# A second load in channel-by-token layout for the later channel steps of a transformer layer

## The chip, the cores and the metric

The kernel runs on one core of one Trainium2 chip. The metric is device time in microseconds (us) of one execution; the time before is the median of three runs. A profile of one execution shows each engine's instructions: TensorE (PE, with its weight loads as PEld), VectorE (DVE), ScalarE (ACT), GpSimd (POOL), and SyncE (SP), which only issues transfers. 16 DMA engines carry the transfers.

## The reference

One layer of a diffusion backbone in float32: 256 latent tokens `x` and 256 context tokens `ctx`, 2048 channels each. What matters here is the beginning:

```python
m_lat = [m[:, None, :] for m in adaln(c, w_ada[l], b_ada[l])]      # silu(c) @ w_ada + b_ada, six chunks
m_ctx = adaln(c_ctx, w_ada[l], b_ada[l])
hc = modulate(rms_norm(ctx, norm1_g[l]), m_ctx[0], m_ctx[1])       # h * (1 + scale) + shift
pc = hc @ w_in_l[:, :KV_WIDTH]                                     # keys and values of the context
h = modulate(rms_norm(x, norm1_g[l]), m_lat[0], m_lat[1])
p = h @ w_in_l                                                     # keys, values, queries, gates
```

`rms_norm` multiplies each token by its own reciprocal root of the mean square, and each channel by a gain. `modulate` multiplies each channel by 1 + scale and adds shift; both depend on the channel and on whether the token is latent or context, not on the token. After this come two kinds of attention, gates, an output projection and a SwiGLU block, which the change does not touch.

## The kernel before, in words

Tokens stand in four blocks of 128: blocks 0 and 1 are context, 2 and 3 latent. Channels stand in 16 tiles of 128 (`kt`). Products are made in three passes (`mm3`, L211 to L214): each float32 operand is split into a rounded part `hi` and a rest `lo`, and hi·hi, hi·lo and lo·hi are added up. For the product the channels must lie on the partitions, so each token tile is turned.

**Loads (L93 to L96).** `tok_in[q]` holds 512 channels of all four blocks, token by channel. SP's queue also carries every weight load: `load_w` (L198 to L209) loads two tiles of 128 rows into a `wraw` buffer, ACT rounds it to `whi` (L207), DVE makes the rest `wlo` (L208). `ada_cond` (L251 to L289) loads 512 KB pieces of `w_ada` (`wada`), multiplies them on PE with 32 columns (L268), and gives scale and shift of some channel tiles. `wraw` and `wada` share seven buffers, so SP waits when all seven are in use.

**Startup (L524 to L541).** For each block in the order 2, 3, 0, 1: `row_norm` (L131) sums squares on ACT and DVE and lets POOL take the power -0.5 (`rstd_of`, L124 to L129); `row_scale` (L145) multiplies the block's first 512 channels by the result on DVE; channel tile 0 is turned, modulated (`mod_first`) and multiplied with some of `w_in`. Then the other 1536 channels of the block are scaled (L539).

**Steps (L523, L544 to L572).** `steps = [(0, 1), (1, 1), (2, 2), (4, 4), (8, 4), (12, 4)]` are pairs of first channel tile and count. In each step, `kv_group` (L355 to L381) multiplies the step's tiles of all four blocks with six groups of 512 columns of `w_in` (keys and values), adding up in SBUF (L378 on DVE). Between the groups, the scale and shift for the next step are made, and after the last two groups `modulated` (L295 to L320) prepares the next step's channels: PE turns two channel tiles of two blocks into one PSUM tile `xtp` (L309, four transposes), DVE (L314) and ACT (L316) each modulate one tile into `hx`, ACT rounds both (`hi`) and DVE subtracts (`lo`, L218). The latent part goes to `xT`, which stays for the queries and gates, the context part to `cT`. From the last two groups of step 3 on, DVE also adds up other `w_ada` chunks (`ada_pieces`, L395).

**Order.** Buffers come from pools: `big` has 15 tiles of 1 MB (128 x 2048 float32) for `tok_in`, the key and value sums, `xT` and `cT`; `tp` is two PSUM banks for everything that is turned; `scr` three scratch tiles. Each engine runs its queue in order. That order is made at build time by a planner: the text's order is the priority, and an instruction whose inputs and buffers are ready may be placed ahead of earlier ones that still wait. `tc.issue_after(i)` keeps instructions of an engine behind `i`, as for `small_loads` (L548 to L550), which are on POOL's queue.

Of the kernel before, what the change touches and what calls it, by code (L numbers as in the profile page):

```python
# [11 lines left out]
F32 = mybir.dt.float32  # L12
F32R = mybir.dt.float32r
AF = mybir.ActivationFunctionType
ALU = mybir.AluOpType
AX = mybir.AxisListType

P = 128
D = 2048
NKT = D // P  # L20
SEQ = 256
# [13 lines left out]
CG = 512  # L35
# [10 lines left out]
def hybrid_block(ctx: ExitStack, tc: tile.TileContext, t: dict, out: bass.AP):  # L46
    nc = tc.nc
# [3 lines left out]
    tab = ctx.enter_context(tc.tile_pool(name="tab", bufs=1))  # L51
# [5 lines left out]
    def big_tile(name, dt=F32):  # L57
        return big.tile([P, 2048], dt, tag="big", name=name)
# [4 lines left out]
    def tp_ps(name="tp"):  # L63
        return psum.tile([P, CG], F32, tag="tp", bufs=2, name=name)
# [4 lines left out]
    def scratch(name, n=CG, dt=F32, tag="scr", bufs=3):  # L69
        return scr.tile([P, n], dt, tag=tag, bufs=bufs, name=name)  # L70

    def small(name, n):
        return sm.tile([P, n], F32, tag=f"sm{n}", name=name)


    ident = tab.tile([P, P], F32, name="ident")
# [3 lines left out]
    ones = tab.tile([P, 32], F32, name="ones")  # L80
# [40 lines left out]

    last_pow = []

    def rstd_of(ss, n, dim, name, by=1.0):  # L124

        r = small(name, n)
        nc.vector.tensor_scalar(out=r, in0=ss, scalar1=by / dim, scalar2=EPS * by, op0=ALU.mult, op1=ALU.add)
        last_pow.append(nc.gpsimd.tensor_tensor(out=r, in0=r, in1=neghalf[:, 0:n], op=ALU.pow))
        return r  # L129

    def row_norm(i):  # L131
        ssq = small("ss_part", 4)
        for q in range(4):
            xt = tok_in[q][:, i, :]
            junk = scratch("junk", tag="p", bufs=4)
            if q % 2 == 0:
                nc.scalar.activation(out=junk, in_=xt, func=AF.Square, accum_out=ssq[:, q:q + 1])
            else:
                nc.vector.scalar_tensor_tensor(out=junk, in0=xt, scalar=1.0, in1=xt, op0=ALU.mult, op1=ALU.mult,
                                               accum_out=ssq[:, q:q + 1])  # L140
        ss = small("ss_row", 1)
        nc.vector.tensor_reduce(out=ss, in_=ssq, axis=AX.X, op=ALU.add)
        return rstd_of(ss, 1, D, "rstd_row")

    def row_scale(i, r, qs):  # L145
        for q in qs:
            xt = tok_in[q][:, i, :]
            nc.vector.tensor_scalar(out=xt, in0=xt, scalar1=r, scalar2=None, op0=ALU.mult)

    def small_loads():  # L150

        def to_all(dst, nm):
            nc.gpsimd.dma_start(out=dst, in_=t[nm].partition_broadcast(P).rearrange("p l d -> p (l d)"))

        lamv = scratch("lamv", 4 * BD, tag="p", bufs=4).rearrange("p (i c) -> p i c", i=4)
        for i, nm in enumerate(("lam_q1", "lam_q2", "lam_k1", "lam_k2")):
            to_all(lamv[:, i, :], nm)
        gsub = tab.tile([P, BV], F32, name="gsub")
        to_all(gsub, "subln_g")
        gains, cosin = {}, {}  # L160
        for br, hd, tag in (("a", AD, "sq"), ("b", BD, "nr")):
            cosin[br] = scratch("cs", 2 * hd, tag="p", bufs=4).rearrange("p (i w c) -> p i w c", i=2, w=2)
            nc.gpsimd.dma_start(out=cosin[br], in_=t[f"rope_{br}"].rearrange("(i p) w c -> p i w c", p=P))
            gains["k" + br] = tab.tile([P, hd], F32, name=f"g_k{br}")
            gains["q" + br] = scratch("gq", hd, tag=tag, bufs=2)
            for qk in ("q", "k"):
                to_all(gains[qk + br], f"{qk}_norm_{br}")
        return lamv, gsub, gains, cosin
# [47 lines left out]
    def split(hi, lo, src):  # L216
        nc.scalar.copy(out=hi, in_=src)
        nc.vector.tensor_tensor(out=lo, in0=src, in1=hi.bitcast(F32), op=ALU.subtract)  # L218
# [24 lines left out]
    xT = Parts("xT", NKT)  # L243
# [51 lines left out]
    def modulated(k0, nk):  # L295

        shift, scale = cond_of[k0]
        cT = big_tile("cT", F32R).rearrange("p (h k c) -> p h k c", h=2, c=CTX)
        cT_of[k0] = cT
        for w in range(2):  # L300
            for j in range(0, nk, 2):
                tp = tp_ps("xtp")
                hx = scratch("hx")
                m = min(2, nk - j)
                for jj in range(m):
                    kt = k0 + j + jj
                    for i in range(2):
                        c0 = (2 * jj + i) * P
                        nc.tensor.transpose(out=tp[:, c0:c0 + P], identity=ident,  # L309
                                            in_=tok_in[kt // 4][:, i + 2 - 2 * w, (kt % 4) * P:(kt % 4 + 1) * P])  # L310
                    sl = slice(jj * SEQ, (jj + 1) * SEQ)
                    s_c, b_c = scale[:, j + jj, w:w + 1], shift[:, j + jj, w:w + 1]
                    if jj == 0:
                        nc.vector.tensor_scalar(out=hx[:, sl], in0=tp[:, sl], scalar1=s_c, scalar2=b_c, op0=ALU.mult, op1=ALU.add)  # L314
                    else:
                        nc.scalar.activation(out=hx[:, sl], in_=tp[:, sl], func=AF.Identity, scale=s_c, bias=b_c)  # L316
                kt = k0 + j
                v, k = (xT.tile4(kt // 4), kt % 4) if w == 0 else (cT, j)
                split(v[:, 0, k:k + m, :], v[:, 1, k:k + m, :], hx[:, 0:m * SEQ].rearrange("p (k c) -> p k c", k=m))
                yield None  # L320

    firsts, last_first = {}, []

    def keep_busy(n):

        idle = mm_ps("idle")
        with tc.issue_after(last_pe[0].ins):
            for _ in range(n):
                nc.tensor.transpose(out=idle[:, 0:P], in_=ident, identity=ident)
# [18 lines left out]
    def kv_first(tok, cg):  # L348
        (hi, lo), (wh, wl) = firsts[tok], ws0[cg]
        nm, idx = kv_of[cg]  # L350
        ps = mm_ps()
        last_pe[0] = mm3(ps, hi, lo, wh[:, 0], wl[:, 0], True, True)
        nc.scalar.copy(out=acc[nm][idx][:, tok * CG:(tok + 1) * CG], in_=ps)
# [136 lines left out]
    def take(gen, n):  # L490
        for _ in range(n):
            if next(gen, gen) is gen:
                return

    def drain(gen):
        for _ in gen:
            pass
# [32 lines left out]
    for tok, todo in ((2, ((2, 2),)), (3, ((3, 2), (2, 3), (3, 3), (2, 0), (3, 0))), (0, ((0, 2), (0, 3), (0, 0))), (1, ((1, 2), (1, 3), (1, 0)))):  # L530
        r = row_norm(tok)
        row_scale(tok, r, (0,))
        if tok >= 2:
            keep_busy(16 if tok == 2 else 8)
        mod_first(tok)
        if tok >= 2:
            keep_busy(10)
        with tc.issue_after(last_first[-1].ins):
            row_scale(tok, r, (1, 2, 3))  # L539
        for of in todo:  # L540
            kv_first(*of)  # L541
    later = ada_later()
    later_keys = iter(())
    for si, (k0, nk) in enumerate(steps):  # L544
        last = si == len(steps) - 1
        nxt = iter(()) if last else ada_cond(*steps[si + 1])
        mod = iter(()) if last else modulated(*steps[si + 1])
        if si == 2:  # L548
            with tc.issue_after(last_pow[3].ins):
                lamv, gsub, gains, cosin = small_loads()  # L550
        if si == 4:
            with tc.issue_after(last_lo[-1].ins):
                lambdas()
            tables()
        if last:
            later_keys = keys("b", 0)
        for n, cg in enumerate((2, 3, 0, 4, 5, 1)):
            if si == 0 and cg in ws0:
                continue
            for half, _ in enumerate(kv_group(si, k0, nk, cg)):  # L560
                if half == 0 and n in BATCH[si]:
                    take(nxt, 1)
                if si == 3 and n >= 4:
                    take(later, 2)
                elif si > 3:
                    take(later, 1)
                if last and n > 0:
                    take(later_keys, 1)
            if n >= 4:
                drain(nxt)  # L570
                take(mod, 2)
        drain(mod)  # L572
# [144 lines left out]
    def unit(br, u):  # L717
        return (u // 4, u % 4) if br == "a" else (u // 8, u // 2 % 4)
# [59 lines left out]
    for n, (br, u) in enumerate(units):  # L778
        q = (br, unit(br, u)[0])
# [33 lines left out]
    for cg in range(4):  # L813
        m, gs = [], []
# [194 lines left out]
```

## Time and profile before

| what | value |
| --- | --- |
| median of 3 runs | 1733.82 us (1732.61 to 1733.86) |
| span of the profiled execution, first to last instruction | 1730.7 us |
| time outside that span, against the median | 3.1 us |
| PE busy, share of the span | 1706.1 us, 99% |
| DVE busy | 1132.6 us, 65% |
| ACT busy | 775.0 us, 45% |
| DMA moved | 397.69 MB, mean 230 GB/s |
| transposes of the changed steps | 48, between 109.8 and 273.8 us |

The span runs from the first to the last instruction of the profiled execution; the runs' time also holds what lies around it. Busy time of PE is modelled at its end, so the start of one instruction to the start of the next is the better price of an instruction there. "idle before" names the time an engine did nothing, and what ended it. A stretch in the tables is given in us from the span's start.

### The profile page before, as it was taken

Reading aid. Unit: us, or ns where it says so; the run is one execution under the profiler, and the core shown is the slowest. Engines: PE = TensorE matmul, PEld = TensorE weight load, DVE = VectorE, ACT = ScalarE, POOL = GpSimd, SP = SyncE. Lnnn points to the kernel's source line nnn. Section 1 sums busy time; section 2 is a strip of 40 time slices with the busy share of each in tenths; the row PEclk is TensorE's granted clock in tenths of the full one; section 3 lists DMA queues with packets and bytes.
Section 4 is the critical chain, followed back from the end, with each engine's and each line's share of the span. In section 5 each row is a group of like instructions: output and inputs, shape, how many; then the busy total and the mean of one; then the engine's idle time right before and its main releaser. Section 6 shows DMA issues by size and latency. Waiting matters only on the chain.

```text
span 1730.7 us, 21827 instructions
## 1 busy us (share of the span) xinstructions
PE 1706.1 (99%) x8150; PEld 1378.5 (80%) x8150; DVE 1132.6 (65%) x1428; ACT 775.0 (45%) x1063; POOL 135.5 (8%) x204
## 2 busy tenths in 40 slices
PE   7999999999999999999999999999999999999998
PEld 5667778887787788888888788888888888888887
DVE  5754668888788879796665754555565665454554
ACT  5222223245656556667544444444444444333332
POOL 2100001001131120002110100000000000000000
PEclk9999999999999999999999999999999999999999
DMA  9877785687766676777796766677777777666662
GB/s 263 300 242 265 233 319 174 201 271 235 252 189 202 212 265 217 247 227 248 249 323 222 237 180 190 201 237 241 234 242 234 240 236 231 208 213 197 221 205 88
DMA packets 192010, 397.69 MB, mean 230 GB/s; under 512 B 13504, under 2 KB 25872, under 8 KB 191392
## 3 DMA queue, kind: packets, MB, share of 16 engines
q1 hardware_dynamic: 183952, 369.71, 66.2%
q0 software_dynamic: 7952, 26.58, 4.8%
q8 instruction: 64, 1.05, 0.2%
q14 instruction: 42, 0.34, 0.1%
HBM read 385.72 MB, written 10.52 MB: 229 GB/s over the span
## 4 chain that ended last, share of the span: by engine, by line
PE 88%; DVE 5%; issue 3%; DMA 1%; ACT 1%; POOL 1%; SPq 0%; DVEq 0%; ACTq 0%; POOLq 0%
PE mm L212 26%; PE mm L213 26%; PE mm L214 26%; PE ada L268 2%; DVE wlo L208 1%; PE ptp L687 1%; PE o L705 1%; DMA wraw<-in_w_in_dram 1%; PE ftp L951 1%; PE s L667 1%; ACT whi L207 1%; PE o L213 0%; PE o L214 0%; PE o L212 0%; PE s L212 0%
## 5 line engine op out<-in xcount | busy, mean ns | idle before, releaser
L208 DVE TENSOR_TENSOR wlo<-wraw,whi 128x1024 fp32r<-128x1024 f32 (+1 forms) x506 | 611.6, 1210 | 460.2 <-ACT whi L207 458.8
L207 ACT CAST whi<-wraw 128x1024 fp32r<-128x1024 f32 (+1 forms) x506 | 527.7, 1043 | 796.6 <-PE mm L214 682.0
L213 PE MATMUL mm<-wlo,hT 128*128 128x512 f32 x696 | 271.0, 389 | 2.0 <-DVE wlo L208 2.0
L212 PE MATMUL mm<-whi,hT 128*128 128x512 f32 x696 | 272.8, 392 | 0.0
L214 PE MATMUL mm<-whi,hT 128*128 128x512 f32 x696 | 271.3, 390 | 0.1
L212 PE MATMUL mm<-whi,xT 128*128 128x512 f32 x640 | 257.2, 404 | 0.6 <-ACT whi L207 0.6
L213 PE MATMUL mm<-wlo,xT 128*128 128x512 f32 x640 | 251.5, 393 | 0.9 <-DVE wlo L208 0.9
L214 PE MATMUL mm<-whi,xT 128*128 128x512 f32 x640 | 250.5, 392 | 0.0
L213 PEld LDWEIGHTS mm<-wlo,hT 128*128 128x128 f32 x696 | 130.7, 188 | 28.8 <-DVE wlo L208 2.4
L214 PEld LDWEIGHTS mm<-whi,hT 128*128 128x128 f32 x696 | 130.6, 188 | 27.9 <-DVE hT L218 0.5
L395 DVE SCALAR_TENSOR_TENSOR ada<-wada,sc,ada 128x1024 f32<-128x1024 f32 x120 | 152.0, 1277 | 0.0
L212 PEld LDWEIGHTS mm<-whi,hT 128*128 128x128 f32 x696 | 130.7, 188 | 26.3
L212 PEld LDWEIGHTS mm<-whi,xT 128*128 128x128 f32 x640 | 120.1, 188 | 37.3 <-issue 9.8
L213 PEld LDWEIGHTS mm<-wlo,xT 128*128 128x128 f32 x640 | 120.8, 189 | 25.1 <-DVE wlo L208 2.4
L214 PEld LDWEIGHTS mm<-whi,xT 128*128 128x128 f32 x640 | 120.3, 188 | 25.4
L212 PE MATMUL mm<-whi,fT 128*128 128x512 f32 x352 | 137.2, 390 | 0.0
L214 PE MATMUL mm<-whi,fT 128*128 128x512 f32 x352 | 137.0, 389 | 0.0
L213 PE MATMUL mm<-wlo,fT 128*128 128x512 f32 x352 | 136.9, 389 | 0.0
L212 PEld LDWEIGHTS mm<-whi,fT 128*128 128x128 f32 x352 | 66.1, 188 | 14.5 <-issue 0.8
L212 PE MATMUL mm<-whi,cT 128*128 128x512 f32 x192 | 75.5, 393 | 1.8 <-ACT cT L344 1.8
L214 PEld LDWEIGHTS mm<-whi,fT 128*128 128x128 f32 x352 | 66.1, 188 | 13.9
L213 PEld LDWEIGHTS mm<-wlo,fT 128*128 128x128 f32 x352 | 66.1, 188 | 13.4
(237 smaller groups left out, 2115.2 us busy)
## 6 DMA issues: line engine op xcount, KB each, us to landing
wada<-in_w_ada_dram SPq DMA_DIRECT2D x192, 512.0 KB, 4.6
wraw<-in_w_in_dram SPq DMA_DIRECT2D x154, 512.0 KB, 4.6
wraw<-in_w_ff_gate_dram SPq DMA_DIRECT2D x88, 512.0 KB, 4.5
wraw<-in_w_ff_up_dram SPq DMA_DIRECT2D x88, 512.0 KB, 3.8
wraw<-in_w_ff_down_dram SPq DMA_DIRECT2D x88, 512.0 KB, 4.8
wraw<-in_w_br_a_dram SPq DMA_DIRECT2D x32, 512.0 KB, 5.0
wraw<-in_w_out_dram SPq DMA_DIRECT2D x32, 512.0 KB, 5.1
wraw<-in_w_br_b_dram SPq DMA_DIRECT2D x16, 512.0 KB, 5.4
```

The source lines that it names most:

```text
L207: last_hi.append(nc.scalar.copy(out=hi[:, 0:nk], in_=raw[:, 0:nk]))
L208: last_lo.append(nc.vector.tensor_tensor(out=lo[:, 0:nk], in0=raw[:, 0:nk], in1=hi[:, 0:nk].bitcast(F32), op=ALU.subtract))
L212: nc.tensor.matmul(ps, lhsT=ah, rhs=wh, start=first, stop=False)
L213: nc.tensor.matmul(ps, lhsT=ah, rhs=wl, start=False, stop=False)
L214: return nc.tensor.matmul(ps, lhsT=al, rhs=wh, start=False, stop=last)
L268: last_pe[0] = nc.tensor.matmul(aps[32 * g:32 * g + 32, 0:ncol], lhsT=cst[:, k, :], rhs=rhs, start=(k < 4), stop=(k >= NKT - 4))
L395: nc.vector.scalar_tensor_tensor(out=dst, in0=wt, scalar=sc[:, 0, kt:kt + 1], in1=dst, op0=ALU.mult, op1=ALU.add)
L667: nc.tensor.matmul(sps[i], lhsT=qT[rows, x, hh, tk * P:(tk + 1) * P], rhs=kT["b", grp][y][rows, hh, :], start=(n == 0), stop=(n == 2))
L687: nc.tensor.transpose(out=tp[:, kt * P:(kt + 1) * P], in_=p[:, kt * P:(kt + 1) * P], identity=ident)
L705: nc.tensor.matmul(op[:, 0:BV], lhsT=pT[:, kt, :], rhs=vb[:, kt, hh * BV:(hh + 1) * BV], start=(kt == 0), stop=(kt == 3))
L951: nc.tensor.transpose(out=tp[:, j * P:(j + 1) * P], in_=act[tk][:, j * P:(j + 1) * P], identity=ident)
```

## The change

Channels 512 to 2047 (steps 3, 4 and 5) no longer come from `tok_in` by transposes. On the host the arrays `x_t` and `ctx_t` are laid out channel by token (a copy, no arithmetic), and `load_turned` fetches them as `tok_t[1]` to `tok_t[3]`, each with two loads of 512 KB on SP's queue. The reciprocal roots of all tokens, until now one number per partition, are spread along the free axis: `spread_rstd` puts each block's 128 numbers on a diagonal, and products with ones write every token's number to all partitions. In `modulated` these steps then take, per channel tile and pair of blocks, one DVE operation z = tok_t * scale * r, one ACT operation hi = z + shift, and one DVE operation lo = (z + shift) - hi. The scaling of channels 512 to 2047 in the startup goes away. `tok_in` is still loaded whole, for the sums of squares, and channels 0 to 511 are as before.

```diff
+    r_tok = tab.tile([P, 4], F32, name="r_tok")
+
-    def rstd_of(ss, n, dim, name, by=1.0):
+    def rstd_of(ss, n, dim, name, by=1.0, r=None):
-        r = small(name, n)
+        r = small(name, n) if r is None else r
...
-        return rstd_of(ss, 1, D, "rstd_row")
+        return rstd_of(ss, 1, D, "rstd_row", r=r_tok[:, i:i + 1])
...
+    r_of = []
+
+    def spread_rstd():
+
+        r_all = big_tile("r_all")[:, 0:4 * P].rearrange("p (i c) -> p i c", i=4)
+        r_of.append(r_all)
+        diag = scratch("diag")
+        for i in range(4):
+            nc.vector.tensor_scalar(out=diag[:, i * P:(i + 1) * P], in0=ident, scalar1=r_tok[:, i:i + 1], scalar2=None, op0=ALU.mult)
+        ps = tp_ps("r_all")
+        for g in range(4):
+            nc.tensor.matmul(ps[32 * g:32 * g + 32, :], lhsT=ones, rhs=diag, start=True, stop=True)
+        nc.scalar.copy(out=r_all, in_=ps.rearrange("p (i c) -> p i c", i=4))
+
+    tok_t = {}
+
+    def load_turned(q):
+
+        tok_t[q] = big_tile(f"tok_t{q}").rearrange("p (i k c) -> p i k c", i=4, c=P)
+        for i, nm in ((2, "x_t"), (0, "ctx_t")):
+            nc.sync.dma_start(out=tok_t[q][:, i:i + 2], in_=t[nm][q - 1].rearrange("p i (k c) -> p i k c", c=P))
...
-                tp = tp_ps("xtp")
                 hx = scratch("hx")
                 m = min(2, nk - j)
+                if k0 >= 4:
+                    kt, i0 = k0 + j, 2 - 2 * w
+                    v, k = (xT.tile4(kt // 4), kt % 4) if w == 0 else (cT, j)
+                    for jj in range(m):
+                        z = hx[:, jj * SEQ:(jj + 1) * SEQ]
+                        s_c, b_c = scale[:, j + jj, w:w + 1], shift[:, j + jj, w:w + 1]
+                        nc.vector.scalar_tensor_tensor(out=z.rearrange("p (i c) -> p i c", i=2), in0=tok_t[kt // 4][:, i0:i0 + 2, kt % 4 + jj, :],
+                                                       scalar=s_c, in1=r_of[0][:, i0:i0 + 2, :], op0=ALU.mult, op1=ALU.mult)
+                        hi, lo = [v[:, x, k + jj, :] for x in range(2)]
+                        nc.scalar.activation(out=hi, in_=z, func=AF.Identity, bias=b_c)
+                        nc.vector.scalar_tensor_tensor(out=lo, in0=z, scalar=b_c, in1=hi.bitcast(F32), op0=ALU.add, op1=ALU.subtract)
+                    yield None
+                    continue
+                tp = tp_ps("xtp")
...
-        with tc.issue_after(last_first[-1].ins):
-            row_scale(tok, r, (1, 2, 3))
...
+        if si == 1:
+            spread_rstd()
+        if 1 <= si < 4:
+            load_turned(si)
...
+    for nm in ("x", "ctx"):
+        turned = given[nm].reshape(2, P, NKT // 4, 4, P).transpose(2, 4, 0, 3, 1)[1:]
+        given[nm + "_t"] = np.ascontiguousarray(turned).reshape(3, P, 2, CG)
```

## The prediction

> **What bounds the kernel now.** I read the page first, then the busy time of the engines by stretches, then the transposes (tile `xtp`) and who waits for them, then the SP queue and the DMA rates of the first 75 us, where the new loads must go.
>
> ```profile
> span 1730.7 us, 21827 instructions
> PE 1706.1 (99%) x8150; PEld 1378.5 (80%) x8150; DVE 1132.6 (65%) x1428; ACT 775.0 (45%) x1063; POOL 135.5 (8%) x204
> PE 88%; DVE 5%; issue 3%; DMA 1%; ACT 1%; POOL 1%; SPq 0%; DVEq 0%; ACTq 0%; POOLq 0%
> ```
>
> TensorE is busy 99% of the span and holds 88% of the chain that ended last. So what leaves PE's stream shortens the kernel by about its own length, if its inputs keep up. The change touches only the first 280 us, and there two stages differ. Columns of the next rows: stretch, its length, busy us and instructions of PE, PEld, DVE, ACT and POOL, granted clock, DMA share, GB/s.
>
> ```profile
> 20.00:25.00 5.00, 2.62 (x19) 2.40 (x16) 4.42 (x14) 3.15 (x8) 0.95 (x1) 0.84 1.06 383
> 30.00:35.00 5.00, 3.62 (x34) 2.64 (x35) 3.65 (x13) 3.31 (x8) 3.70 (x7) 1.00 1.06 210
> 35.00:40.00 5.00, 5.00 (x29) 3.57 (x28) 2.68 (x5) 4.28 (x9) 3.75 (x6) 1.00 0.81 109
> 45.00:50.00 5.00, 4.94 (x24) 3.79 (x24) 4.02 (x9) 2.76 (x6) 5.00 (x20) 1.00 1.08 366
> 50.00:55.00 5.00, 5.00 (x47) 3.25 (x46) 3.38 (x6) 1.61 (x3) 0.73 (x4) 1.00 0.34 102
> 60.00:65.00 5.00, 4.21 (x30) 2.84 (x23) 3.67 (x7) 2.21 (x5) 0.00 (x0) 1.00 1.01 348
> 105.00:123.00 18.00, 18.00 (x89) 14.08 (x87) 14.29 (x23) 7.35 (x12) 0.00 (x0) 1.00 0.78 263
> 175.00:201.00 26.00, 25.82 (x120) 19.90 (x119) 20.97 (x33) 8.31 (x13) 0.00 (x0) 1.00 0.73 227
> 256.00:276.00 20.00, 20.00 (x99) 16.23 (x98) 17.36 (x26) 7.50 (x11) 2.04 (x4) 1.00 0.74 243
> ```
>
> From 105 us on PE is full and the DMA engines have a quarter of their time left. Before 65 us the DMA engines are full in most slices (share about 1.0), and PE waits now and then: 0.8 us are missing from 60 to 65. The chain there passes through a weight load:
>
> ```profile
> 54.44 6.22 DMA wraw<-in_w_in_dram
> 60.66 0.02 issue
> 60.68 0.63 ACT whi L207
> 61.31 0.02 issue
> 61.33 0.70 DVE wlo L208
> ```
>
> A byte more ahead of this load is a later start of PE at 61 us. Two holes stand against that: 109 GB/s from 35 to 40 and 102 GB/s from 50 to 55, where SP had nothing to issue.
>
> **Transposes off PE.** Steps 3, 4 and 5 (channels 512 to 2047) lose 12 x 4 transposes.
>
> ```profile
> L309 PEld LDWEIGHTS xtp<-ident,tok x48: 138/140/143, 109.8 to 273.8; 128*128 128x128 f32 x48
> L314 DVE TENSOR_SCALAR hx<-xtp,mod,mod x12: 531/536/544, 111.0 to 272.9; 128x256 f32<-128x256 f32 x12
> L316 ACT ACTIVATE hx<-xtp,mod,mod x12: 554/562/567, 112.1 to 274.7; 128x256 f32<-128x256 f32 x12
> ...
>   PEld xtp L309: 1.6, 4
> ```
>
> ```profile
> 116.21 0.58 PEld L309 LDWEIGHTS xtp<-ident,tok 128*128 128x128 f32 x4
> 116.77 0.19 PEld L212 LDWEIGHTS mm<-whi,xT 128*128 128x128 f32 x1
> ```
>
> Four of them hold PE's stream from 116.21 to 116.77, so one is 0.14 us, and 48 are 6.7 us. The median weight load of 140 ns says the same. Beside it go the 1.6 us that transposes waited until DVE's `hx` freed their PSUM buffer. PE: **-8.3 us**, which is also the most that these rows hold; if the waits only move to the next matmul and as much again lay in gaps, it is 6.7 - 1.6 = 5.1.
>
> **The spread reciprocal root.** It adds four 32-column f32 matmuls of 512 columns, the same form as the row sum of L412, four small DVE scalings of the identity and one ACT copy.
>
> ```profile
> 342.94 1.00 PE adac L412 x8
> ```
>
> Eight instructions (two passes of four) are 1.0 us of PE: **+1.0 us**, between 0 (they fall into PE's idle 1.4 us from 30 to 35) and 1.5 (PE also waits for the scaled identities).
>
> **DVE and ACT.** Columns: line, engine, operation, count, busy us, mean ns, idle before.
>
> ```profile
> L674 DVE SCALAR_TENSOR_TENSOR p<-p,rs 128x512 f32<-128x512 f32 x16 | 12.0, 747 | 4.4 <-ACT p L673 4.3
> L445 DVE TENSOR_TENSOR nr<-nr,sq 128x256 f32<-128x256 f32 x18 | 7.4, 413 | 0.0
> L148 DVE TENSOR_SCALAR tok<-tok,rstd_row 128x512 f32<-128x512 f32 x16 | 7.1, 493 | 1.6 <-POOL rstd_row L128 1.6
> L218 DVE TENSOR_TENSOR cT<-hx,cT 128x512 fp32r<-128x512 f32 (+1 forms) x8 | 5.2, 660 | 0.9 <-ACT cT L217 0.9
> L443 DVE TENSOR_TENSOR sq<-mm,rp_qa 128x512 f32<-128x512 f32 x8 | 5.5, 681 | 0.0
> ```
>
> A scalar_tensor_tensor of 256 is not in the trace. Halving a 512 one takes off what halving a tensor_tensor takes off (681 - 413 = 268 ns), so 747 - 268 = 0.48 us; bounds 0.41 (L445) and 0.75 (L674). The change issues 48: 23.0 us. It takes away 12 scalings out of PSUM (12 x 0.536) and 12 differences (12 x 0.68), 14.6 us. So each of the three step ends gets 2.8 us more of DVE. In the stretch from 175 to 201, which also carries the `ada` products, DVE has 5.0 of 26 us left; from 105 to 123 it has 3.7 of 18, from 256 to 276 2.6 of 20. In the first two it fits, in the last it is 0.2 over, and a `wlo` queued behind these operations would stop PE. I take **+0.8 us** (bounds 0 and 3 x 2.8 = 8.4, were none of it covered); nearer 0, since the new products no longer wait for transposes that PE does late, and can be taken into DVE's gaps earlier. ACT loses: 12 x (0.56 + 0.6) become 24 activations of at most 0.56. [...]
>
> Three row scalings per token block leave DVE's startup (12 x about 0.42).
>
> ```profile
> 19.04 1.27 DVE L148 TENSOR_SCALAR tok<-tok,rstd_row 128x512 f32<-128x512 f32 x3
> 20.22 0.69 DVE L139 SCALAR_TENSOR_TENSOR junk<-tok 128x512 f32<-128x512 f32 x1
> ```
>
> ```profile
> PE xtp L339 <- DVE tok L148: 3.0, 2, 2.4
> ```
>
> The squares of the next block start the moment the three scalings end, and PE waits 2.4 us for that block. So PE is 1.2 us earlier at 23 us, and perhaps spared part of its slow clock there. But by 61 us PE waits for a load, not for its own past. I count **0**; the bound is -2.0, these 1.2 and the (1 - 0.84) x 5 = 0.8 us of lost clock from 20 to 25.
>
> **The loads.** Six of 512 KB, 3.15 MB; at the 366 GB/s of 45 to 50 us that is 8.6 us of all 16 engines, 1.43 each. They are asked for at steps 1, 2 and 3, on the SP queue, but nothing in the kernel ties them to that place: they need only a free `big` buffer. What is ready is pulled ahead:
>
> ```profile
> 31.84 1.47 POOL L153 DMA_DIRECT2D lamv<-in_lam_q_dram  x2
> ...
> 41.90 2.74 POOL L182 TENSOR_TENSOR rp_qa<-cs,gq 128x64 f32<-128x64 f32 x8 [2.94 <-DMA gq<-in_q_norm_a_dram]
> ```
>
> Both come from code written at steps 2 and 4, and run before step 1. And SP has times when its next load waits for a buffer, as within the 9.74 us that four issues took here:
>
> ```profile
> 37.52 4.68 SPq L260 DMA_DIRECT2D wada<-in_w_ada_dram  x4
> 43.37 1.14 SPq L200 DMA_DIRECT2D wraw<-in_w_in_dram  x2
> 44.60 9.74 SPq L260 DMA_DIRECT2D wada<-in_w_ada_dram  x4
> ```
>
> So I expect the six loads to stand between about 20 and 45 us, before the weights of step 1. Queued behind them are the `wada` and `wraw` of steps 0 and 1; ACT's `whi` and DVE's `wlo` wait for these, and PE for them. From 30 to 40 the slices fall short of 366 GB/s by 156 and 257, for 5 us each: 2.1 MB of room, worth 5.6 us; part of it is blocked, since the small POOL loads clog that time (share 0.81 at 109 GB/s). If all of the room is used, 3.0 us of the 8.6 stick out; if none, 8.6; if the loads stay at their steps, those of step 1 lie in the hole and those of steps 2 and 3 in stretches with DMA time to spare, for about 0. I take **+2.7 us**, close to the room-used case, with the range from 0 to 8.6.
>
> **Sum.** -8.3 + 1.0 + 0.8 + 0 + 2.7 = -3.8 us. It is made against the profiled span of 1730.7 us, which becomes 1726.9. The median of the runs, 1733.82, is 3.1 us above that span (what lies around it); I carry the same 3.1 over: **1730.0 us**.
>
> **Rivals.**
> *The loads are hidden* (in the holes, or late enough at their steps): no DMA term, -6.5, 1727.3 us. For it: 2.1 MB of room at 30 to 40 and the 102 GB/s from 50 to 55. Against it: the slices with share above 1.0 on both sides, and that the second hole is itself SP waiting for a late `wlo`.
> *The gain is given back*: the loads cost 5 us instead of 2.7, and DVE's extra work at the crowded step end 2 instead of 0.8, so -8.3 + 1.0 + 5 + 2 = -0.3, 1733.5 us. For it: 20.97 busy of 26 us on DVE, and 0.81 of DMA share in the hole. Or the transposes were cheap to begin with, being tucked into PE's gaps (5.1 us instead of 8.3).
> *Slower: a cold start.* All six loads go ahead of step 1's `wada`, and the hole does not take them: 8.6 us. PE, whose stream has these products in order, then idles over 2.4 us near 35 us, and the granted clock halves for about 3 us, as it did after the 2.4 us wait (0.84 as the mean of 20 to 25), which costs 1.5 more: 8.6 + 1.5 - 6.5 = +3.6, 1737.4 us. It decides from 6.5 us of exposed transfer. For it: the pulling ahead shown above. Against it: the room at 30 to 40. [...]
>
> **How the numbers follow.** Chances: forecast (1728.5 to 1731.5) 0.40, hidden 0.20, given back 0.25, slower 0.15. A measurement tells 0.2% from no change, 3.5 us, so faster means below 1730.3: of the forecast 0.24 lies below and 0.16 above. Faster 0.24 + 0.20 = 0.44, same 0.16 + 0.25 = 0.41, slower 0.15. The range from 1726.5 to 1736.5 leaves out the slower rival and little else.
>
> **What would show it.** Right: no `xtp` on PE after 75 us; the six loads issued on SP before 45 us; a weight load that ends PE's wait near 61 us later than 60.7; step 3's matmuls starting some 3 us late and step 5 ending 3 to 5 us early; DVE's stretch near 175 to 201 close to full. Wrong: the loads standing at steps 1 to 3 in SP's order (then hidden), PE waiting over 1 us for `wlo` or `cT` at a step end (given back), a granted clock below 1 after 30 us (slower). A shift of the later stages, which the change does not touch, would make all of it wrong.

## The result and the profile after

The kernel after takes 1724.77 us (median of five runs, 1722.47 to 1727.13) against 1733.82 us before: a ratio of 0.995, with a 95% interval from 0.9938 to 0.9962, or 9.05 us less. The direction was predicted; the time lies 1.7 us below the range and 5.2 us below the forecast.

The page of after: span, busy time of the engines, shares of the chain of waits.

```profile
span 1725.0 us, 21768 instructions
PE 1697.9 (98%) x8110; PEld 1370.6 (79%) x8110; DVE 1134.0 (66%) x1444; ACT 772.9 (45%) x1064; POOL 134.1 (8%) x204
PE 85%; DVE 5%; issue 3%; DMA 3%; ACT 1%; POOL 1%; SPq 1%; ACTq 0%; DVEq 0%; POOLq 0%
```

PE stays the bound, with 8.2 us less work. This profiled execution is the slowest of the five; it took 1727.13 us, so 2.1 us lie around its span. Stretches of after, with the same columns as before:

```profile
20.00:25.00 5.00, 4.20 (x25) 3.13 (x23) 3.83 (x11) 4.02 (x11) 0.63 (x2) 1.00 1.06 381
45.00:50.00 5.00, 4.65 (x26) 2.44 (x28) 2.09 (x7) 2.39 (x6) 4.63 (x20) 1.00 1.08 373
50.00:55.00 5.00, 5.00 (x47) 3.58 (x40) 5.00 (x9) 1.19 (x3) 0.00 (x0) 1.00 0.97 343
175.00:201.00 26.00, 26.00 (x125) 20.13 (x124) 21.22 (x41) 6.89 (x12) 0.00 (x0) 1.00 0.60 193
256.00:276.00 20.00, 20.00 (x89) 16.54 (x89) 19.57 (x33) 6.52 (x11) 2.03 (x4) 1.00 0.63 220
```

Four things differ from before. From 20 to 25 us PE is busy 4.20 us, not 2.62, at full clock. The hole of the DMA engines from 50 to 55 us (102 GB/s before) is filled. PE no longer lacks time from 175 to 201. And DVE is full from 256 to 276 (19.57 of 20 us) without PE losing anything.

SP's queue of after, where the first pair of the new loads went (start, length, line, operation):

```profile
42.23 0.64 SPq L284 DMA_DIRECT2D wada<-in_w_ada_dram  x1
42.92 1.88 SPq L172 DMA_DIRECT2D tok_t<-in_x_t_dram  x1
44.85 0.43 SPq L172 DMA_DIRECT2D tok_t<-in_ctx_t_dram  x1
50.56 1.48 SPq L284 DMA_DIRECT2D wada<-in_w_ada_dram  x3
```

Behind the pair SP issued nothing for 5.3 us: its next load had to wait, in the end for a `wlo` on DVE that gives back one of the seven shared buffers. So the pair was issued, and most of its transfer ran, while no weight load could have been issued; it landed some 9 us after its issue (medians 9.5 and 8.9 us), a little after SP went on. The other pairs went out at 72 and 106 us, at their steps.

To follow the lead I use one tile, `kb`, whose sums are added up on DVE from step 1 to step 5; first and last start are the two times behind the durations. Before:

```profile
L378 DVE TENSOR_TENSOR kb<-mm,kb x40: 677/691/693, 49.1 to 297.6; 128x512 f32<-128x512 f32 x40
```

and after:

```profile
L415 DVE TENSOR_TENSOR kb<-mm,kb x40: 675/683/693, 46.3 to 290.2; 128x512 f32<-128x512 f32 x40
```

After leads by 2.8 us at 46 us and by 7.4 us at 290 us. So in these two profiles 2.8 us come out of startup and step 0, and 4.6 us out of the steps. A second profile of each (`before_again`, `after_again`, below) shows how far this holds:

```profile
L378 DVE TENSOR_TENSOR kb<-mm,kb x40: 677/691/693, 48.1 to 296.9; 128x512 f32<-128x512 f32 x40
L415 DVE TENSOR_TENSOR kb<-mm,kb x40: 676/684/692, 45.9 to 289.0; 128x512 f32<-128x512 f32 x40
```

There the lead is 2.2 us at 46 us and 7.9 us at 289 us.

### The profile page after: what moved, and what is told of

It is laid out like the page before. It is cut to its first block, busy times and chain, and to the rows that moved or that the text cites. A ratio compares the mean times of both kernels' runs of the same rounds, so it can differ in the third digit from the quotient of the medians.

```text
span 1725.0 us, 21768 instructions
## 1 busy us (share of the span) xinstructions
PE 1697.9 (98%) x8110; PEld 1370.6 (79%) x8110; DVE 1134.0 (66%) x1444; ACT 772.9 (45%) x1064; POOL 134.1 (8%) x204
## 4 chain that ended last, share of the span: by engine, by line
PE 85%; DVE 5%; issue 3%; DMA 3%; ACT 1%; POOL 1%; SPq 1%; ACTq 0%; DVEq 0%; POOLq 0%
PE mm L237 26%; PE mm L236 26%; PE mm L238 26%; DMA wraw<-in_w_in_dram 3%; DVE wlo L232 2%; PE ptp L726 1%; PE ada L292 1%; ACT whi L231 1%; PE o L744 1%; PE ftp L990 1%; PE s L706 1%; PE o L237 0%; PE o L238 0%; PE o L236 0%; PE s L236 0%
## 5 line engine op out<-in xcount | busy, mean ns | idle before, releaser
L236 PEld LDWEIGHTS mm<-whi,xT 128*128 128x128 f32 x640 | 119.5, 188 | 40.7 <-issue 11.4
```

What stands on the lines that cost most here:

```text
L236: nc.tensor.matmul(ps, lhsT=ah, rhs=wh, start=first, stop=False)
```

## The experiments

The kernel before ran beside each group; its medians were 1733.1 to 1734.3 us there, its single runs 1730.7 to 1737.6 us. Between two medians, under about 1.5 us says little. Line numbers shift by a few from kernel to kernel.

**The transposes alone** (`no_turns`, made from before).

```diff
...
                 for jj in range(m):
...
+                    if k0 >= 4:
+                        src = tok_in[kt // 4][:, 2 - 2 * w:4 - 2 * w, (kt % 4) * P:(kt % 4 + 1) * P]
...
-                        nc.vector.tensor_scalar(out=hx[:, sl], in0=tp[:, sl], scalar1=s_c, scalar2=b_c, op0=ALU.mult, op1=ALU.add)
+                        nc.vector.tensor_scalar(out=dst, in0=src, scalar1=s_c, scalar2=b_c, op0=ALU.mult, op1=ALU.add)
```

> The kernel before, with the 48 transposes left out: DVE and ACT modulate the token-by-channel tiles as they are (so channels 512 to 2047 are computed from numbers in the wrong place). No second loads, no spread root, scalings of the startup as before, DVE's operations as many as before. Prediction's term for the transposes with the waits at them: 8.3 us, 1725.5 us. The price that turns_back showed, 3.4 us by the medians to 5.2 us by the profiles: 1728.5 to 1730.4 us.

1724.22 us, ratio 0.9947 (0.9934 to 0.9959): 8.9 us less than the kernel before beside it. Its `kb`:

```profile
L384 DVE TENSOR_TENSOR kb<-mm,kb x40: 677/691/693, 49.1 to 291.5; 128x512 f32<-128x512 f32 x40
```

No lead at 49 us, 6.1 us at 291 us. The prediction's term of 8.3 us lies inside the interval of the medians (7.1 to 11.4 us); the profile shows less at the place of the transposes. From the first `kb` to the last it takes 242.4 us, against 248.5 and 248.8 us in the two profiles of before: 6.1 to 6.4 us. Some waits went away too. They show at the end of step 3, in the list of what PE's weight loads waited for (us in total, times, longest). Before, 184 to 206 us:

```profile
PEld ada L268 <- issue: 1.3, 4, 0.4
PEld mm L214 <- DVE cT L218: 0.8, 1, 0.8
PEld mm L212 <- issue: 0.8, 1, 0.8
PEld xtp L309 <- DVE hx L314: 0.6, 1, 0.6
PEld mm L212 <- ACT cT L217: 0.4, 1, 0.4
```

After, 181 to 200 us:

```profile
PEld ada L292 <- issue: 0.9, 3, 0.4
PEld mm L236 <- issue: 0.8, 1, 0.8
```

The waits for `hx` and `cT` are gone; at the ends of steps 2, 3 and 4 together they were 3.3 us in before.

**The transposes put back** (`turns_back`, from after).

```diff
+                    tp = tp_ps("xtp")
+                    for c in range(2 * m):
+                        nc.tensor.transpose(out=tp[:, c * P:(c + 1) * P], identity=ident, in_=tok_t[kt // 4][:, i0 + c % 2, kt % 4 + c // 2, :])
+                    nc.scalar.activation(out=small("turned", 1), in_=tp[:, 0:1], func=AF.Identity,
+                                         scale=scale[:, j, w:w + 1], bias=shift[:, j, w:w + 1])
```

> The kernel after with the 48 transposes added again at their place (each set of four is read by one small ACT operation that depends on the scale; nothing else uses them). Prediction's price, 48 x 0.14 = 6.7 us and 1.6 us of waits: 1731.5 to 1733.1 us. Price by start-to-start in the trace of before, 48 x 0.12 = 5.9 us and no waits: 1730.7 us. If the transposes lay in gaps: 1724.8 us.

1728.24 us, 3.4 us slower than after; ratio to before 0.9965 (0.9954 to 0.9977).

```profile
L420 DVE TENSOR_TENSOR kb<-mm,kb x40: 678/690/693, 46.1 to 295.5; 128x512 f32<-128x512 f32 x40
```

At 295 us it is 5.3 us behind after, about what 48 transposes take on PE at 0.12 us each (5.8). The transposes are back here, but nothing on the path waits for their output, and the waits for `hx` and `cT` stay away. By the medians, putting the transposes back (3.4 us) costs less than taking them out brings (8.9 us), and those waits could be the reason. The profiles do not show it: from the first `kb` to the last, taking them out saves 6.1 to 6.4 us and putting them back costs 5.5 us against after and 6.3 us against `after_again`. Both are close to the transposes' own time on PE. So what the waits were worth is not shown.

**The startup** (`scale_back`, from after; `scale_late`, from before).

```diff
+        with tc.issue_after(last_first[-1].ins):
+            row_scale(tok, r, (1, 2, 3))
```

> The kernel after, with the twelve row scalings of channels 512 to 2047 put back into the startup (their results are not used). Startup theory: these scalings held back the next block's squares, so some 3 to 4 us of the gain come from their removal; the time is 1728 to 1729 us, PE waits over 2 us before a transpose of the startup and the granted clock falls below 0.9 between 20 and 30 us. Prediction's theory (startup worth 0, because PE waits for a load at 61 us anyway): within 1 us of the 1724.8 us of the kernel after, and the lead of 3 us at 30 us is gone by 65 us with or without them.

```diff
-        with tc.issue_after(last_first[-1].ins):
-            row_scale(tok, r, (1, 2, 3))
...
+        if si in (1, 2, 3):
+            with tc.issue_after(last_lo[-1].ins):
+                for tok in (2, 3, 0, 1):
+                    row_scale(tok, r_tok[:, tok:tok + 1], (si,))
```

> The kernel before, with transposes, without the second loads, but the twelve scalings are taken out of the startup and done at the beginnings of steps 1, 2 and 3 (four in each, behind the weights' rests on DVE). Startup theory: 3 to 4 us faster than before, 1730 to 1731 us. Prediction's theory: 1733.8 us within 1 us, as the startup is worth nothing.

`scale_back` takes 1726.27 us, 1.4 and 1.5 us more than after's two medians; `scale_late` 1732.40 us, ratio 0.999 (0.9981 to 0.9999), 1.2 us less than before. Both point to about 1.3 us: under half of the startup theory, and hardly more than the differences between medians that say little. `kb` of `scale_back`, then of `scale_late`, and the stretch of `scale_back` from 20 to 25 us:

```profile
L415 DVE TENSOR_TENSOR kb<-mm,kb x40: 679/691/693, 47.9 to 291.2; 128x512 f32<-128x512 f32 x40
L380 DVE TENSOR_TENSOR kb<-mm,kb x40: 680/689/693, 46.3 to 297.3; 128x512 f32<-128x512 f32 x40
```

```profile
20.00:25.00 5.00, 2.62 (x19) 2.13 (x18) 4.41 (x14) 2.98 (x8) 0.95 (x1) 1.00 1.06 383
```

`scale_back` is 1.6 us behind after at 48 us and still 1.0 us at 291 us. `scale_late` starts `kb` 2.8 us earlier than before, but of that only 0.3 us are left at 297 us, and against `before_again` nothing; its scalings, moved into the steps, may have cost the rest. So the profiles do not settle between the prediction's 0 and about 1.3 us. In `scale_back` the clock did not fall, against the expectation: PE is busy as long as in before, at 1.00 instead of 0.84.

**The kernel before once more** (`before_again`, no edit).

> The kernel before once more, for a second profile. Its first profile had a granted clock of 0.5 from 24 to 26.6 us behind a wait of 2.6 us on PE, while scale_back had the same wait and no fall of the clock. If the fall belongs to the kernel, it is there again and the lead of scale_back over this profile is again 1.3 us at 30 us; if it is a matter of the single execution, it may be missing, and so is that lead.

```profile
20.00:25.00 5.00, 2.62 (x21) 2.20 (x20) 4.41 (x14) 3.22 (x8) 0.95 (x1) 1.00 1.06 382
```

The same kernel with the same idle time, and no fall of the clock (1731.55 us, span 1729.4). `no_turns`, which has the startup of before, waits the same 2.4 us there, and its clock falls in the next stretch:

```profile
25.00:30.00 5.00, 4.67 (x15) 3.39 (x14) 3.04 (x10) 3.26 (x7) 0.86 (x1) 0.72 1.16 308
```

So with this startup the clock falls in some executions and not in others: here in two of four profiles (before and `no_turns`, but not `before_again` and `scale_back`). What decides between the two, no run here shows.

**Without the loads** (`no_loads`, from after).

```diff
...
-                                                       in0=tok_t[kt // 4][:, i0:i0 + 2, kt % 4 + jj, :],
+                                                       in0=tok_in[kt // 4][:, i0:i0 + 2, (kt % 4 + jj) * P:(kt % 4 + jj + 1) * P],
...
-        if 1 <= si < 4:
-            load_turned(si)
```

> The kernel after without the six loads: the new products read the same amount from the token-by-channel tiles instead (so channels 512 to 2047 are computed from wrong numbers). Prediction's theory (loads cost 2.7 us): 1722.1 us. Loads that are hidden at their steps: 1724.8 us within 1 us, although the trace should be up to 2 us earlier near 55 us.

1726.90 us, ratio 0.9962 (0.9948 to 0.9975): 2.1 us slower than after, which neither side expected. So where they stand in after, leaving the loads out gives nothing back. Some of the loss stands at the end of step 2, from 103 to 124 us, in waits that after does not have:

```profile
PEld mm L236 <- ACT cT L337: 0.9, 1, 0.9
...
PEld mm L236 <- DVE va L415: 0.6, 1, 0.6
```

There the planner had ordered ACT's and DVE's queues otherwise. An order can cost as much as the effect that is looked for, so this run alone cannot tell a free load from one that costs a little. The traces speak for little or nothing: from 46 to 65 us PE's weight loads wait for `whi` and `wlo` 1.0 and 1.3 us in the two profiles of after, 2.0 and 0.6 us in the two of before.

**The loads elsewhere** (`loads_twice`, `all_step1`, `at_step0`, `early`, all from after).

```diff
+        again = big_tile(f"again{q}").rearrange("p (i k c) -> p i k c", i=4, c=P)
+        for dst in (tok_t[q], again):
```

> The kernel after with each of the six loads issued a second time, into another big buffer that nobody reads. If the loads at their steps cost 2.7 us: 1727.5 us. If they are hidden: 1724.8 us within 1 us, with at most 2 us less lead at 60 us, won back by 75 us. If they cost their full transfer time of 8.6 us: 1733.4 us.

```diff
-        if 1 <= si < 4:
-            load_turned(si)
+        if si == 1:
+            for q in (1, 2, 3):
+                load_turned(q)
```

> The kernel after with all six loads asked for at step 1, in one row where after has the first two. SP's hole there is 5.3 us long and after's first pair uses 2.6 us of transfer. If a load costs what sticks out of the hole: 8.6 - 5.3 = 3.3 us, 1728.1 us. If place does not matter: 1724.8 us within 1.5 us. If all of the four moved loads count in full: 5.7 us, 1730.5 us.

```diff
+        if si == 0:
+            for q in (1, 2, 3):
+                load_turned(q)
...
-        if 1 <= si < 4:
-            load_turned(si)
```

> The kernel after with all six loads asked for at the beginning of step 0, behind the startup. They then stand on SP's queue behind the second wada piece of that time, ahead of the weights of steps 0 and 1, which is the place the prediction expected, and ACT's order in the startup stays that of the kernel after (in early it did not: there ACT's hi of a latent block stood behind squares of the context, which cost PE 5.7 us and the clock). If the transfers alone made early slow: over 1735 us. Prediction's price for this place: 2.7 us, up to 8.6 and 1.5 for the clock: 1727.5 to 1735 us. If weights there wait for buffers anyway: at most 1726.3 us.

In `early` the three calls stand right behind the token loads.

> The kernel after with all six loads issued on SP right behind the token loads, ahead of every weight load of the steps (the place that the prediction expected). Prediction's price: 3.0 us if the thin stretch from 30 to 40 us takes its share, 8.6 us if not, and 1.5 more for a halved clock: 1727.5 to 1735 us, with PE waiting over 2 us between 30 and 45 us. Buffer theory (the weight loads there wait for one of seven buffers that PE must free, not for the transfers ahead of them): under 2 us, at most 1726.8 us.

| kernel | median us | against after |
| --- | --- | --- |
| after, pairs at steps 1, 2, 3 | 1724.8 | |
| `loads_twice` | 1729.26 | +4.4 |
| `all_step1` | 1731.66 | +6.9 |
| `at_step0` | 1736.15 | +11.3 |
| `early` | 1740.61 | +15.8 |

So the same loads can be left out for no gain in one place and cost many us in another. `loads_twice` is well above its case for hidden loads, and `all_step1` above all three of its cases. SP's hole at step 1 gets four loads there, or six, instead of two, and what is issued behind them lands late. The weight load that took 5.95 us in after (below) takes 9.59 us in `loads_twice`, and PE in `all_step1` is busy 2.98 of 5 us from 60 to 65 us, with the clock at 0.67:

```profile
52.03 9.59 DMA wraw<-in_w_in_dram
```

```profile
60.00:65.00 5.00, 2.98 (x27) 1.01 (x28) 0.00 (x0) 1.00 (x3) 0.00 (x0) 0.67 1.06 379
```

`at_step0` is the place the prediction expected, and there the change is slower than before: ratio 1.0014 (1.0005 to 1.0022). Its SP queue, the waits of PE's weight loads from 24 to 45 us, and two stretches:

```profile
21.61 1.47 SPq L172 DMA_DIRECT2D tok_t<-in_x_t_dram  x1
...
25.96 0.33 SPq L172 DMA_DIRECT2D tok_t<-in_ctx_t_dram  x1
26.73 0.38 SPq L284 DMA_DIRECT2D wada<-in_w_ada_dram  x1
28.49 4.90 SPq L224 DMA_DIRECT2D wraw<-in_w_in_dram  x1
```

```profile
PEld ada L292 <- DMA wada<-in_w_ada_dram: 5.7, 1, 5.7
...
PEld mm L236 <- ACT whi L231: 1.9, 2, 1.6
```

```profile
35.00:40.00 5.00, 1.59 (x7) 0.96 (x6) 0.00 (x0) 2.15 (x4) 1.81 (x3) 1.00 0.93 230
40.00:45.00 5.00, 1.97 (x18) 1.15 (x19) 0.81 (x1) 0.78 (x2) 1.80 (x5) 0.53 0.93 246
```

PE waits 5.7 us for the `wada` behind the loads, is busy 1.59 of 5 us, and then the clock falls to 0.53. Its first `kb` starts at 55.9 us, 9.6 us behind after, so most of the loss lies here. This is the prediction's *slower* rival, place and clock, at 11.3 us instead of its 10.1. `early` has besides another order on ACT (a startup `hi` behind squares that wait for token loads), so its 15.8 us are not the loads' alone.

**The spread** (`no_spread`, `spread_dma`, `spread_row`, from after).

```diff
...
-        ps = tp_ps("r_all")
-        for g in range(4):
-            nc.tensor.matmul(ps[32 * g:32 * g + 32, :], lhsT=ones, rhs=diag, start=True, stop=True)
...
+        nc.gpsimd.memset(r_all, 1.0)
```

> The kernel after without the spreading: the tile of spread roots is filled with ones by POOL (so channels 512 to 2047 miss their normalisation), and no small transfer is added. If the products with their waits, 1.7 us of PE's stream near 46 us, reach the end: 1723.2 us. If PE meets the same late weights at 59 us with or without them: 1724.8 us. In both cases the lead over the kernel before at 50 us should be 1.7 us larger than in the kernel after.

1724.56 us: 0.2 to 0.3 us less than after, which is nothing. Yet in after the products hold PE's stream near 46 us (the wait ahead of each group in brackets):

```profile
46.45 0.19 PEld L163 LDWEIGHTS r_all<-diag,ones 128*32 128x32 f32 x8 [0.75 <-PE mm L238]
47.48 0.19 PEld L236 LDWEIGHTS mm<-whi,xT 128*128 128x128 f32 x1 [0.84 <-ACT va L413]
```

Without them PE meets transfers that have not landed (`no_spread`, 46 to 62 us):

```profile
PEld mm L230 <- ACT whi L225: 1.8, 2, 1.2
PEld ada L286 <- DMA wada<-in_w_ada_dram: 1.6, 1, 1.6
```

So leaving the products out gave nothing back: PE waits for late weights instead, the clock falls (0.66 from 60 to 65 us), and the last `kb` starts at 292.6 us, 2.4 us behind after. That the spread hides behind loads in after fits this; by itself it is not shown, since the order of the loads is another one too. Two ways to take it off PE were slower. `spread_dma` hands the roots out through DRAM; `spread_row` turns them on PE first, so that the store has four rows.

```diff
...
+        nc.gpsimd.dma_start(out=r_d.rearrange("i p -> p i"), in_=r_tok)
+        nc.gpsimd.dma_start(out=flat, in_=r_d.rearrange("(l i) c -> l (i c)", l=1).partition_broadcast(P).rearrange("p l d -> p (l d)"))
```

> The kernel after, with the reciprocal roots spread by a store of 2 KB to DRAM and a load that hands it to all partitions, on POOL's queue: the eight PE instructions, the four DVE scalings of the identity and the ACT copy go away. Prediction's price of the spread, 1.0 us: 1723.8 us. Price read from the trace of after, with the wait ahead of the products (0.7 us) and the one behind them (0.9 us): 1.0 + 1.6 = 2.6 us, 1722.2 us. If PE loses this lead again at the weights near 59 us: 1724.8 us.

```diff
...
+        nc.tensor.transpose(out=ps[0:4, 0:P], in_=r_tok, identity=ident)
+        nc.scalar.copy(out=r_sb, in_=ps[0:4, 0:P])
+        nc.gpsimd.dma_start(out=r_d, in_=r_sb)
```

> The kernel after; the reciprocal roots are turned by one small transpose (4 x 128), copied by ACT, stored to DRAM as four rows of 512 bytes and handed to all partitions by a second transfer. Eight PE instructions become one, and the store no longer has 512 pieces of four bytes as in spread_dma, whose store took 10.9 us with the weights behind it late. Spread priced with its waits at 2.6 us: 1722.3 us. Spread priced at 1.0 us: 1723.8 us. If the small transfers again hold back the weights: 1726 to 1727 us.

1727.09 us and 1727.71 us. In `spread_dma` the store lands late; its row among the issues (KB, us from issue to landing):

```profile
r_d<-r_tok POOLq DMA_DIRECT2D x1, 2.0 KB, 10.9
```

That this store makes the weights late is not shown: three loads of 32 to 128 KB on the same queue also take 10.2 to 10.7 us in that run, and 7.0 to 8.4 us in after. In `spread_row` it is SP's queue, with PE's waits from 50 to 66 us:

```profile
42.18 8.32 SPq L285 DMA_DIRECT2D wada<-in_w_ada_dram  x2
50.56 0.50 SPq L173 DMA_DIRECT2D tok_t<-in_x_t_dram  x1
```

```profile
PEld ada L293 <- DMA wada<-in_w_ada_dram: 6.1, 2, 3.5
PEld atp L302 <- ACT asb L297: 1.4, 1, 1.4
```

The first pair stands behind one more `wada`, which waits for a buffer. It misses the hole and goes out 7.6 us later than in after, together with the weights, and PE waits 7.5 us. No line of the edit asks for that; the planner did it.

**Less DVE work at the step ends** (`pool_norm`, from after).

```diff
+                nc.gpsimd.tensor_tensor(out=v, in0=v, in1=r_of[0][:, i0:i0 + 2, :], op=ALU.mult)
...
+                        nc.vector.tensor_scalar(out=z.rearrange("p (i c) -> p i c", i=2), in0=y, scalar1=s_c, scalar2=b_c, op0=ALU.mult, op1=ALU.add)
+                        nc.scalar.activation(out=hi.rearrange("p (i c) -> p i c", i=2), in_=y, func=AF.Identity, scale=s_c, bias=b_c)
+                        nc.vector.tensor_tensor(out=lo, in0=z, in1=hi.bitcast(F32), op=ALU.subtract)
```

> The kernel after; POOL, idle from 50 to 250 us, multiplies the turned loads by the spread roots in place ahead of time. Then ACT takes hi straight from the turned load, and DVE's scalar_tensor_tensor from three inputs becomes a tensor_scalar, so each step end has less DVE work and a shorter chain. If DVE's queue at the step ends still costs PE time: 1722 to 1723.5 us. If these step ends are covered (prediction: +0.8 us for all of DVE's extra work): 1724 to 1725 us. If POOL and DVE hinder each other: above 1726 us, with DVE operations longer between 75 and 130 us.

1725.21 us, the same as after. Its last `kb` starts at 292.0 us, 1.8 us behind after, so its steps gained nothing from the shorter DVE work: the step ends were covered. None of these kernels beats after.

**After once more** (`after_again`, no edit).

> The kernel after once more. 1724.8 us within 1.5 us. Its first profile lost about 3 us of its lead between 736 and 966 us, where the change has no part: if that was one execution, this profile ends near 1722 us; if it is a new order of the later stages, it loses the same again.

1724.91 us, span 1722.6 in its profile. Against before, with DVE's and ACT's instructions matched one by one, the first profile of after loses 1.8 us of its lead for good near 805 us (from 7.3 to 5.5 us), this one 0.2 us (from 8.1 to 7.9). The 3 us of the expectation also hold a shift near 966 us that both profiles make up again. So most of the loss was one execution.

## Why the prediction was wrong

| step | predicted, us | the runs, us |
| --- | --- | --- |
| transposes and their waits | -8.3 | -8.9 by medians (`no_turns`, -7.1 to -11.4 by its interval), -6.1 and -6.4 between first and last `kb` |
| startup | 0, bound -2.0 | -1.2 and -1.4 by medians, not settled by the profiles |
| spread | +1.0 | none given back without it (`no_spread`) |
| DVE at the step ends | +0.8 | none seen (`pool_norm`) |
| six loads | +2.7 | none given back at their steps (`no_loads`); +11.3 where I put them |
| sum | -3.8 | -9.05 |

The largest term was about right by the medians. Costs of 4.5 us, set against it, did not show.

- **The step that failed**: "So I expect the six loads to stand between about 20 and 45 us." They went out at 43, 72 and 106 us. The ground given (they need only a free `big` buffer) did not suffice: `early` issues all six between 20 and 26 us, so there were buffers, and still the planner left them at their steps. What held them there, unlike the small loads of POOL's queue, no run shows. And the price was wrong for the place: I took 2.7 us, near the low end, where `at_step0` shows 11.3. The two errors made a number that fits neither. The case named last there, loads at their steps for about 0, is what happened: the *hidden* rival, whose 1727.3 us is still 2.5 us too high.
- **The transposes**: 0.14 us each was read from one set of four; all 48 together hold the stream of weight loads of before for 5.9 us, 0.12 each, not 6.7. With the 1.6 us of waits for `hx` that is 7.5 us, and the waits for `cT` were left out. The profiles' 6.1 to 6.4 us lie between the term's lower case of 5.1 and its 8.3.
- **The spread** was sized right by itself (8 in 1.0 us), but of its range from 0 to 1.5 the lower end is what `no_spread` supports.
- **The startup**: "by 61 us PE waits for a load, not for its own past" takes the load for independent of PE. The chain of after into that wait:

```profile
50.45 1.88 DVE kb L415 x3
52.33 0.61 DVE wlo L232
52.94 0.02 issue
52.96 5.95 DMA wraw<-in_w_in_dram
```

  The load goes out when a `wlo` frees its buffer, and that stands behind additions of PE's sums. An earlier PE can so give an earlier load (52.96 us, against 54.44 in the chain of before), and part of the lead can survive. Nor was the wait at 61 us there in every execution: in `before_again`, whose clock did not fall, PE is busy 5.00 of 5 us from 60 to 65. How much of the lead survives is open (0 to about 1.3 us, see the startup runs). The other part of the bound, the lost clock, came in two profiles of four with this startup.
- **DVE**: 0.48 us for an operation was right, but in a row they overlap. Groups of after up to 285 us (busy us, mean ns of one, idle before):

```profile
L334 DVE SCALAR_TENSOR_TENSOR hx<-tok_t,mod,r_all 128x256 f32<-128x256 f32 x24 | 10.3, 477 | 0.1
L338 DVE SCALAR_TENSOR_TENSOR cT<-hx,mod,cT 128x256 fp32r<-128x256 f32 x12 | 5.4, 473 | 0.0
L338 DVE SCALAR_TENSOR_TENSOR xT<-hx,mod,xT 128x256 fp32r<-128x256 f32 x12 | 5.2, 477 | 0.0
```

  They fill 20.9 us, not 23.0, and a DVE at 19.57 of 20 us kept PE full.
- **The signs**: no `xtp` after 75 us and step 5 early (by more than the 3 to 5 us) came as said. Only the first of the three pairs went out before 45 us; a later weight load at 61 us and a late step 3 did not come. DVE became nearly full from 256 to 276 us, and not where the sign was set: from 175 to 201 us it is busy 21.22 of 26 us, 20.97 before. The sign for *hidden*, loads at steps 1 to 3, came.
- **Around the span**: of the 3.1 us that I carried over, 2.1 lie around it. The rest was a profiled execution faster than the median.

One thing stays open. At 290 us the profiles show after 7.4 us and `no_turns` 6.1 us ahead; the medians say 9.1 and 8.9. Behind the last `kb` the change does nothing, and yet from its start to the end of the span the profiles take 1433.1 and 1432.5 us (before), 1434.8 and 1433.6 us (after) and 1431.5 us (`no_turns`). Part of that is the clock: PE waits 2.0 us near 990 us in every profile, and behind it the clock is 0.66 from 995 to 1000 us in before, while in `no_turns` it stays at 1.00. So one profile each cannot say where the rest of the medians' difference lies.

## What to carry to other kernels

Price an instruction on the bounding engine from all of its instances: 48 transposes were 5.9 us of PE's stream, and the profiles gained 6.1 to 6.4 us without them and lost 5.5 to 6.3 us with them put back, while medians alone said 8.9 and 3.4. A load's price is its place in the issuing queue: the same six gave nothing back when left out from where the queue stood waiting for buffers, and cost 11 us ahead of weights that PE needed next; so look up where a planner put them before pricing, and if you cannot, price each place by itself and not a mean of them. When the bounding engine waits for a load, ask what that load's issue had waited for before calling it independent.

## What the runs showed of the hardware

- The same wait of 2.4 us on PE near 22 us (busy 2.62 of 5 us from 20 to 25) was followed by a lower clock in two profiles (before: 0.84 from 20 to 25 us and 0.82 from 25 to 30; `no_turns`: 0.72 from 25 to 30) and by a full clock in two others (`before_again` and `scale_back`: 1.00 from 20 to 30 us).
- A wait of 2.0 us on PE near 990 us stands in all seventeen profiles; the clock halved behind it for 3.4 us in eight, before (0.66 from 995 to 1000 us) and both of after among them (0.69 from 990 to 995 us in the first), and not in the other nine.
- A store of 2 KB took 10.9 us from issue to landing among weight loads (`spread_dma`), and 1.7 us in another layout and 19 us later (`spread_row`); no run here shows which of the two made the difference.
- POOL took 0.83 us for a multiplication of 128 x 256 in `pool_norm`, DVE 0.48 us in after for an operation with three inputs of that size.
